# State updates of an mLSTM decoder kernel by whole units: four products of 32 rows in place of four with masked keys

## The chip, the cores and the metric

The kernel runs on one NeuronCore of a Trainium2 chip. Its time is the device time of one execution in microseconds; the median of several runs is compared. TensorE (matmuls and weight loads), VectorE, ScalarE, GpSimdE and SyncE each work through a queue of their own in order; the orders are fixed when the kernel is compiled. Results of matmuls land in PSUM, which has eight banks of 128 partitions by 512 fp32 values.

## What is computed

One inference step of a decoder with two layers, a short gated convolution and an mLSTM block, for a prompt of 512 tokens and for 8 sample sequences of 8 tokens, all in fp32. What matters here is the matrix memory of the sample sequences. Each of the 8 sequences and 4 heads has a state C of 512 x 512. In one step of 8 tokens it becomes

```python
decay = jnp.exp(g + m - m_new)
kw = kj * jnp.exp(logw - m_new[..., None])[..., None]
C_new = decay[..., None, None] * C + jnp.einsum('bhjd,bhje->bhde', kw, vj)
```

and the output of the step needs the product of the queries with the old state, `einsum('bhid,bhde->bhie', qj, C)`. That is 32 states of 1 MB to be read, used, updated and written back.

## The kernel before

**Layout.** Tokens of the samples are stacked in 32-row groups: of a head's 8 sequences, four make one half u (0 or 1), and each of the four has 32 partitions, g = 0 to 3. The 8 tokens of a sequence stand there four times, as high and low parts of key and value, so that one matmul over 32 rows gives a product of fp32 precision out of operands in a rounded fp32 format (`stack`, `value_stack`, `key_stack`). A unit (h, u, dt) is 128 of the 512 rows of C for the four sequences of a half; there are 4 x 2 x 4 = 32 units, in the order of heads 2, 0, 1, 3.

**Products.** The stationary operand has all 128 partitions, thus four sequences at once. To have one sequence alone, `key_stack` (L1166) makes four masked copies `km` of the weighted keys on ScalarE, each with one group's rows kept and the others zeroed (L1181 and L1182). `piece` (L1210) takes half a unit, two sequences: per sequence one matmul of 128 rows into a bank `r` (L1235), then one VectorE instruction that multiplies the old state by its decay and adds the bank (L1236).

**Banks.** In the last stage four PSUM banks (tag `b1`, handed out by `bank`, L133) serve these products, the query products, the decay scores (`d`), the transposes of a head's output (`ha`, `hb`) and small sums (`pn`, `qn`). Four more make the two wide accumulators of the large products.

**Queries.** `query_state` (L853) multiplies the queries with the old states: four matmuls of 32 columns each per unit (L859), which accumulate over a head's 8 units in one bank `qa`. Heads 3, 0 and 1 are done earlier in the kernel; head 2 is done in the last stage, each unit ahead of its update.

**Order.** The pieces stand in a queue, `stream`. `tick` (L195) is told of TensorE's time by the large products (0.735 us a step of eight, 0.7 in the numerators and final states) and issues a piece whenever 3.45 us have gathered. Around the pieces run the products with the gate weights `z`, the numerators, the final states of the prompt, and the output projection; their weights come by SyncE's queue, ScalarE rounds them (`wh`, L215) and VectorE computes the remainder (`wl`, L216), into four buffers each of half a chunk. A planner with a cost model fixes each engine's order from this program; instructions in a block of high priority go first when they are ready.

**Transfers.** States come in halves of 512 KB into six buffers (tag `C`). A piece issues the load of the second half after it (`load_half`, L1190; SyncE, L178) and, behind its first update, the store of the half before (`store_half`, L1200; L1205). SyncE's queue also holds the weights' loads (L221) and the other fetches (L1147).

Of the kernel before, what the change touches and what calls it, by code (L numbers as in the profile page):

```python
# [40 lines left out]
CST = {}  # L41
_n = 0
for _name, _cnt in (("ident", 128), ("ones", 128), ("causal", 128), ("smask", 256), ("sel", 64),
                    ("seln", 4), ("gmask", 4), ("k_low", 1), ("v_low", 1), ("v_one", 2)):
# [13 lines left out]
FH = 2  # L58
SECOND = tuple(range(2, 16))
FI = 1  # L60
EARLY = 3.45
NEARLY = 10
SLOTS = {}
WARM = 28
KEEP = 3
# [2 lines left out]
def trunk(tc, io):  # L68
    nc = tc.nc
    ctx = ExitStack()  # L70
    with ctx:
# [103 lines left out]
        def later_load(**kw):  # L175

            with tc.issue_after(latest[0]):
                load(**kw)  # L178
# [16 lines left out]
        def tick(us):  # L195

            if clock[1] is not None:
                clock[0] += us
                while stream and clock[0] >= clock[1]:
                    clock[0] -= clock[1]  # L200
                    stream.popleft()[1]()
                    if len(stream) == 64 - NEARLY:
                        clock[1] = PACE

        def weight_tile():
# [647 lines left out]
        def query_state(st, ct, i):  # L853

            u, dt = divmod(i, 4)
            if i == 0:
                st["q"] = bank("qa")
            for g in (2, 3, 0, 1):
                nc.tensor.matmul(st["q"][32 * g:32 * g + 32, :],  # L859
                                 st["qp"][dt // 2][:, dt % 2, 128 * u + 32 * g:128 * u + 32 * g + 32],  # L860
                                 ct[g // 2][:, g % 2, :], start=(i == 0), stop=(i == 7))
            if i == 7:
                pn = bank("qn")
                nc.tensor.matmul(pn[:, 0:1], st["qn"], c("ones", 0, 1), start=True, stop=True)
                qc = T(513, name="qc")
                nc.scalar.copy(qc[:, 0:512], st["q"])
                nc.vector.tensor_copy(qc[:, 512:513], pn[:, 0:1])
                qcs[st["h"]] = qc

        def scores(st, dt):  # L870
            if dt == 0:
# [294 lines left out]
        def key_stack(h, u):  # L1166

            st = heads[h]
            raw, = fetched.pop(("ks", h, u))
            o = R(512, "kst")  # L1170
            stack(raw, G["s"][:, 1 + u, 32 + 4 * h:33 + 4 * h], c("k_low"), o)
            pn = bank("pn")
            for dt in range(4):
                nc.tensor.matmul(pn[:, 4 * dt:4 * dt + 4], o[:, 128 * dt:128 * dt + 128], seln, start=True, stop=True)
# [3 lines left out]
            nc.vector.tensor_tensor(nst[:, h, u], pn[:, 0:16].rearrange("p (d g) -> p d g", g=4), t, ALU.add)  # L1178

            st[u] = [R(512, "km") for _ in range(4)]  # L1180
            for g, t in enumerate(st[u]):  # L1181
                nc.scalar.activation(t, o.bitcast(F32), AF.Copy, scale=c("gmask", g, g + 1))  # L1182


        ORDER = (2, 0, 1, 3)
        units = [(h, u, dt) for h in ORDER for u in range(2) for dt in range(4)]
        halves = {}
        behind = []

        def load_half(n):  # L1190

            if n < 2 * len(units):
                h, u, dt = units[n // 2]
                i = n % 2
                uid[0] += 1
                t = load_tile("c", "C")
                later_load(out=t, in_=io["cs"][(h * 2 + u) * 4 + dt][:, 2 * i:2 * i + 2])
                halves[n] = t

        def store_half(after=None):  # L1200

            while behind:
                n, t = behind.pop(0)
                h, u, dt = units[n // 2]
                ins = store(out=io["cs_out"][(h * 2 + u) * 4 + dt][:, 2 * (n % 2):2 * (n % 2) + 2], in_=t).ins  # L1205
                if after is not None:
                    tc.add_manual_dep(ins, after.name, mybir.DependencyInfo(mybir.DependencyClass.NoSync,
                                                                            mybir.DependencyReason.DATA))

        def piece(n):  # L1210

            h, u, dt = units[n // 2]
            i = n % 2
            st = heads[h]
            if i == 0:
                if "vst" not in st:
                    value_stack(h)
                if u not in st:
                    key_stack(h, u)
                m = n // 8 + 1  # L1220
                j = (ORDER[m // 2], m % 2) if m < 8 else None
                if dt == 0 and j:
                    fetch(("ks", *j), kss[j[0]][:, j[1], :])
                    if j[1] == 0 and "vst" not in heads[j[0]] and ("vs", j[0]) not in fetched:
                        fetch_stack(j[0])
                if dt == 3 and j:
                    key_stack(*j)
                if h == 2:
                    query_state(st, [halves[n], halves[n + 1]], 4 * u + dt)
            load_half(n + 2)  # L1230
            kst, vst, dec, ct = st[u], st["vst"][u], G["dec"], halves.pop(n)
            o = 8 * h + 4 * u + 2 * i
            for j in range(2):
                r = bank("r")
                nc.tensor.matmul(r, kst[2 * i + j][:, 128 * dt:128 * dt + 128], vst[:, 0:512], start=True, stop=True)  # L1235
                ins = nc.vector.scalar_tensor_tensor(ct[:, j, :], ct[:, j, :], dec[:, o + j:o + j + 1], r,  # L1236
                                                     ALU.mult, ALU.add).ins
                if j == 0:
                    store_half(ins)
            behind.append((n, ct))  # L1240
            if n == 2 * len(units) - 1:
                store_half()

        stream.extend((units[n // 2][0], lambda n=n: piece(n)) for n in range(2 * len(units)))

        def finish(h):
            while any(x[0] == h for x in stream):
# [165 lines left out]
        fetch_stack(0)  # L1413
        fetch_stack(2)
        fetch(("ks", 2, 0), kss[2][:, 0, :])
        load_half(0)
        load_half(1)
# [164 lines left out]
def _consts():  # L1582
# [23 lines left out]
    put("gmask", (g[:, None] == np.arange(4)[None, :]).astype(np.float32))  # L1606
# [112 lines left out]
```

## Time and profile before

| what | value |
|---|---|
| median of 3 runs | 1655.08 us (1655.02 to 1656.1) |
| profiled execution, first to last instruction | 1654.3 us |
| TensorE busy | 1627.4 us, 98% |
| VectorE busy | 1125.8 us, 68% |
| ScalarE busy | 806.9 us, 49% |
| bytes moved | 301.61 MB, 182 GB/s on average |
| first and last product with masked keys | 1295.7 and 1613.0 us |
| products with masked keys | 128 |
| masked copies | 32, 20.7 us of ScalarE |

The page lists a group of instructions as: line, engine, operation, output<-inputs, rows*columns of the stationary operand, shape, count | busy time, mean ns of one | idle time of the engine ahead of them and what ended it. PE is TensorE's matmuls, PEld its weight loads, DVE VectorE, ACT ScalarE, SPq SyncE's queue. The ends of matmuls are modelled and they overlap, so what one costs is read from start to start. A timeline row is: start us, length us, engine, line, operation, tiles, shape, count. An fp32 matmul stands in the records twice, one of the rounded format once.

### The profile page before, as it was taken

To read this page: it belongs to the slowest core of one execution; us is meant where nothing else is said; L and a number is where in the kernel's file an instruction comes from. 1 tells how busy PE (TensorE), PEld (TensorE's weight loads), DVE (VectorE), ACT (ScalarE), POOL (GpSimd) and SP (SyncE) were. 2 spreads that over 40 slices of the span, in tenths; PEclk is the share of its full clock that TensorE was granted. 3 is DMA by queue.
4 is the path that set the end of the run, shared out by engine and by line. 5 is a ranking of instruction groups with operands and counts; after the bars stand their busy time and mean duration, and the time that the engine had idled before them with its cause. 6 is when DMAs were issued, how large, how long until landed. Compare 5 with 4: busy or idle time off the path is not lost. (4 is left out here: it accounts for less than half of the span.)

```text
span 1654.3 us, 31177 instructions
## 1 busy us (share of the span) xinstructions
PE 1627.4 (98%) x12029; PEld 1548.7 (94%) x12029; DVE 1125.8 (68%) x2124; ACT 806.9 (49%) x1622; POOL 148.8 (9%) x295
## 2 busy tenths in 40 slices
PE   9999999999999999999999999999999998999998
PEld 9999999999999999999899989899898787989997
DVE  7988898885337976555966456446458658688775
ACT  5566666653324553434645344344345456556431
POOL 1111111110001000000111010110101000000000
PEclk9999999999999999999999999999999899999999
DMA  6476666654332434535434554454556587998992
GB/s 219 111 174 167 175 168 159 175 136 148 120 120 91 149 121 128 172 119 159 156 103 151 156 177 162 142 188 140 173 190 241 186 280 262 336 341 296 359 342 103
DMA packets 121893, 301.61 MB, mean 182 GB/s; under 512 B 12656, under 2 KB 35056, under 8 KB 121744
## 3 DMA queue, kind: packets, MB, share of 16 engines
q1 hardware_dynamic: 98320, 267.61, 48.7%
q0 software_dynamic: 8064, 14.68, 5.8%
q10 hardware_dynamic: 15360, 17.32, 3.1%
q8 instruction: 94, 1.54, 0.4%
q14 instruction: 55, 0.45, 0.1%
HBM read 235.91 MB, written 63.66 MB: 181 GB/s over the span
## 5 line engine op out<-in xcount | busy, mean ns | idle before, releaser
L345 PE MATMUL p<-hi,wh 128*128 128x288 f32 x1540 | 454.4, 297 | 3.9 <-ACT p L357 1.9
L345 PE MATMUL p<-lo,wh 128*128 128x288 f32 x1540 | 452.6, 294 | 0.0
L345 PE MATMUL p<-hi,wl 128*128 128x288 f32 x1540 | 450.7, 295 | 0.2 <-DVE wl L265 0.2
L345 PEld LDWEIGHTS p<-hi,wh 128*128 128x128 f32 x1540 | 288.5, 188 | 12.7 <-DVE ws L350 4.1
L345 PEld LDWEIGHTS p<-lo,wh 128*128 128x128 f32 x1540 | 289.0, 188 | 0.0
L345 PEld LDWEIGHTS p<-hi,wl 128*128 128x128 f32 x1540 | 287.9, 188 | 0.4 <-DVE wl L265 0.4
L264 ACT CAST wh<-wr 128x512 fp32r<-128x512 f32 (+1 forms) x298 | 171.4, 578 | 215.4 <-PE p L345 123.5
L265 DVE TENSOR_TENSOR wl<-wr,wh 128x512 fp32r<-128x512 f32 (+1 forms) x298 | 185.0, 635 | 94.9 <-ACT wh L264 92.5
L235 PE MATMUL acc<-hi,wh 128*128 128x256 f32 (+1 forms) x1072 | 233.4, 298 | 1.8 <-ACT xm L711 1.0
L235 PE MATMUL acc<-lo,wh 128*128 128x256 f32 (+1 forms) x1072 | 231.9, 297 | 0.0
L235 PE MATMUL acc<-hi,wl 128*128 128x256 f32 (+1 forms) x1072 | 231.7, 297 | 0.0
L264 ACT CAST wh<-ws 128x512 fp32r<-128x512 f32 (+1 forms) x201 | 114.8, 573 | 203.8 <-PE p L345 129.6
L215 ACT CAST wh<-wr 128x512 fp32r<-128x512 f32 x170 | 104.7, 619 | 201.2 <-PE acc L235 148.1
L235 PEld LDWEIGHTS acc<-hi,wh 128*128 128x128 f32 x1072 | 180.4, 190 | 7.4 <-issue 1.6
L216 DVE TENSOR_TENSOR wl<-wr,wh 128x512 fp32r<-128x512 f32 x170 | 116.7, 689 | 98.7 <-ACT wh L215 88.6
L235 PEld LDWEIGHTS acc<-hi,wl 128*128 128x128 f32 x1072 | 179.9, 190 | 1.6 <-issue 1.3
L235 PEld LDWEIGHTS acc<-lo,wh 128*128 128x128 f32 x1072 | 179.9, 190 | 0.6 <-issue 0.2
L265 DVE TENSOR_TENSOR wl<-ws,wh 128x512 fp32r<-128x512 f32 (+1 forms) x201 | 125.5, 630 | 68.7 <-ACT wh L264 68.0
L1236 DVE SCALAR_TENSOR_TENSOR c<-c,cols,r 128x512 f32<-128x512 f32 x128 | 91.5, 743 | 27.0 <-PE r L1235 24.9
L433 PE MATMUL p<-hi,wh 128*128 128x288 f32 x496 | 109.2, 300 | 0.0
L433 PE MATMUL p<-hi,wl 128*128 128x288 f32 x496 | 107.3, 295 | 0.0
L433 PE MATMUL p<-lo,wh 128*128 128x288 f32 x496 | 107.0, 295 | 0.0
(388 smaller groups left out, 2619.1 us busy)
## 6 DMA issues: line engine op xcount, KB each, us to landing
wr<-wts SPq DMA_DIRECT2D x222, 512.0 KB, 3.6
c<-cs SPq DMA_DIRECT2D x112, 512.0 KB, 5.8
cs_out<-c SPq DMA_DIRECT2D x64, 512.0 KB, 7.5
ws<-wts SPq DMA_DIRECT2D x28, 256.0 KB, 4.5
ws<-wts POOLq DMA_DIRECT2D x28, 256.0 KB, 4.7
wr<-wts POOLq DMA_DIRECT2D x28, 256.0 KB, 4.1
x<-xcs SPq DMA_DIRECT2D x20, 288.0 KB, 4.8
x<-xT SPq DMA_DIRECT2D x16, 288.0 KB, 4.3
```

What stands on the lines that cost most here:

```text
L215: last_act[0] = nc.scalar.copy(hi, raw[:, 4 * i:4 * i + 4, :]).ins
L216: nc.vector.tensor_tensor(lo, raw[:, 4 * i:4 * i + 4, :], hi.bitcast(F32), ALU.subtract)
L235: nc.tensor.matmul(acc[:, o:o + j - i], a[:, k % 4, :], x[:, i:j], start=(first and k == 0 and p == 0), stop=(last and k == 7 and p == 2))
L264: last_act[0] = nc.scalar.copy(hi, src).ins
L265: nc.vector.tensor_tensor(lo, src, hi.bitcast(F32), ALU.subtract)
L345: nc.tensor.matmul(bank_, a[:, j, :], x, start=(start and n + j + i == 0), stop=(n == len(groups) - 1 and j == len(g) - 1 and i == 2), ski ...
L433: nc.tensor.matmul(b, a[:, k % 4, :], x[:, t:t + HT], start=bool(start) and k == 0 and i == 0, stop=(k == n - 1 and i == 2), skip_group_ch ...
L1236: ins = nc.vector.scalar_tensor_tensor(ct[:, j, :], ct[:, j, :], dec[:, o + j:o + j + 1], r, ALU.mult, ALU.add).ins
```

## The change

- The masked copies, and the constant that made them, go. `update` replaces `piece` and does a whole unit: four matmuls, one a sequence, whose stationary and moving operands are the 32 partitions of that sequence alone, thus four different row groups of the array, into four banks.
- The four banks are claimed beforehand: VectorE clears the first column of each, in an order kept over all units; every one of the four matmuls waits for the last clear and stands in a block of high priority. Four updates on VectorE follow.
- `query_state` for head 2 no longer accumulates over 8 units in one bank: each unit has a bank of its own, which ScalarE copies for the first unit and VectorE adds for the seven others.
- Loads and stores go by units (two transfers of 512 KB each): a unit issues the load of the next one, and behind its first update the stores of the one before. The pace of the queue is 6.9 us a unit.

```diff
-PACE = 3.45
+PACE = 6.9
-EARLY = 3.45
-NEARLY = 10
+EARLY = 6.9
+NEARLY = 5
...
             u, dt = divmod(i, 4)
-            if i == 0:
+            one = st["h"] not in FAR
+            if i == 0 or one:
                 st["q"] = bank("qa")
             for g in (2, 3, 0, 1):
                 nc.tensor.matmul(st["q"][32 * g:32 * g + 32, :],
                                  st["qp"][dt // 2][:, dt % 2, 128 * u + 32 * g:128 * u + 32 * g + 32],
-                                 ct[g // 2][:, g % 2, :], start=(i == 0), stop=(i == 7))
+                                 ct[g // 2][:, g % 2, :], start=(one or i == 0), stop=(one or i == 7))
+            if i == (0 if one else 7):
+                qcs[st["h"]] = T(513, name="qc")
+                nc.scalar.copy(qcs[st["h"]][:, 0:512], st["q"])
+            elif one:
+                sums = qcs[st["h"]][:, 0:512]
+                nc.vector.tensor_tensor(sums, st["q"], sums, ALU.add)
...
-            st[u] = [R(512, "km") for _ in range(4)]
-            for g, t in enumerate(st[u]):
-                nc.scalar.activation(t, o.bitcast(F32), AF.Copy, scale=c("gmask", g, g + 1))
+            st[u] = o
...
-            load_half(n + 2)
-            kst, vst, dec, ct = st[u], st["vst"][u], G["dec"], halves.pop(n)
-            o = 8 * h + 4 * u + 2 * i
-            for j in range(2):
-                r = bank("r")
-                nc.tensor.matmul(r, kst[2 * i + j][:, 128 * dt:128 * dt + 128], vst[:, 0:512], start=True, stop=True)
-                ins = nc.vector.scalar_tensor_tensor(ct[:, j, :], ct[:, j, :], dec[:, o + j:o + j + 1], r,
-                                                     ALU.mult, ALU.add).ins
-                if j == 0:
-                    store_half(ins)
...
+            cts = held.pop(n)
+            if h == 2:
+                query_state(st, cts, 4 * u + dt)
+            load_unit(n + 1)
+            kst, vst, dec = st[u], st["vst"][u], G["dec"]
+            o = 8 * h + 4 * u
+            rs = [bank("r") for _ in range(4)]
+            for r in rs:
+                with tc.issue_after(last_bank[0]) if last_bank else nullcontext():
+                    last_bank[:] = [nc.vector.memset(r[:, 0:1], 0.0).ins]
+            with tc.high_priority():
+                for g, r in enumerate(rs):
+                    s = slice(32 * g, 32 * g + 32)
+                    mul = nc.tensor.matmul(r, kst[s, 128 * dt:128 * dt + 128], vst[s, 0:512], start=True, stop=True).ins
+                    tc.add_manual_dep(mul, last_bank[0].name, mybir.DependencyInfo(mybir.DependencyClass.Sync,
+                                                                              mybir.DependencyReason.DATA))
+            for g in range(4):
+                ct = cts[g // 2][:, g % 2, :]
+                ins = nc.vector.scalar_tensor_tensor(ct, ct, dec[:, o + g:o + g + 1], rs[g], ALU.mult, ALU.add).ins
+                if g == 0:
+                    store_unit(ins)
+            behind.append((n, cts))
```

More of the change, by code (lines that the diff above doesn't have):

```diff
@@ L864, in query_state @@
                 nc.tensor.matmul(pn[:, 0:1], st["qn"], c("ones", 0, 1), start=True, stop=True)
[L865 to L868, printed above, removed]
+                nc.vector.tensor_copy(qcs[st["h"]][:, 512:513], pn[:, 0:1])
         def scores(st, dt):
@@ L1178, in key_stack @@
             nc.vector.tensor_tensor(nst[:, h, u], pn[:, 0:16].rearrange("p (d g) -> p d g", g=4), t, ALU.add)
-            st[u] = [R(512, "km") for _ in range(4)]
-            for g, t in enumerate(st[u]):
-                nc.scalar.activation(t, o.bitcast(F32), AF.Copy, scale=c("gmask", g, g + 1))
+            st[u] = o
         ORDER = (2, 0, 1, 3)
         units = [(h, u, dt) for h in ORDER for u in range(2) for dt in range(4)]
-        halves = {}
+        held = {}
         behind = []
[L1190 to L1198, printed above, removed]
@@ L1200, in store_half @@
-        def store_half(after=None):
-            while behind:
[L1203 to L1208, printed above, removed]
@@ L1246, in finish @@
+        stream.extend((units[n][0], lambda n=n: update(n)) for n in range(len(units)))
         def finish(h):
```

64 lines of the change are left out of this document (37 added, 27 removed).

## The prediction

> **What bounds the kernel now.** I read the page first: busy shares, then the chain that ended last.
>
> ```profile
> span 1654.3 us, 31177 instructions
> PE 1627.4 (98%) x12029; PEld 1548.7 (94%) x12029; DVE 1125.8 (68%) x2124; ACT 806.9 (49%) x1622; POOL 148.8 (9%) x295
> ...
> PE 20%; DVE 2%; DMA 1%; ACT 1%; issue 0%; DVEq 0%; ACTq 0%
> ```
>
> TensorE is busy 98% of the span, and the part of the chain that could be followed is nearly all TensorE: time taken from TensorE comes off the end, unless another engine fills it again. The other one that shows is VectorE: 2% of the span, 33 us. All the changed work lies in the last stage, from about 1290 us on, so I cut that stage into stretches.
>
> ```profile
> core 0: us, PE busy (x) PEld busy (x) DVE busy (x) ACT busy (x) POOL busy (x), PEclk, DMA share, GB/s
> 1290.00:1410.00 120.00, 113.25 (x721) 92.77 (x720) 79.17 (x159) 64.53 (x142) 4.12 (x13) 0.94 0.75 259
> 1410.00:1530.00 120.00, 116.18 (x834) 110.52 (x833) 94.39 (x187) 69.43 (x145) 6.64 (x15) 0.99 0.92 321
> 1530.00:1610.00 80.00, 79.52 (x578) 76.78 (x577) 59.33 (x110) 31.29 (x60) 1.38 (x2) 1.00 0.98 359
> 1610.00:1654.00 44.00, 36.98 (x285) 35.95 (x283) 24.33 (x61) 7.87 (x18) 0.00 (x0) 0.97 0.31 104
> sum 364.00, PE 345.93 PEld 316.01 DVE 257.23 ACT 173.11 POOL 12.14; mean PE 86.48 PEld 79.00 DVE 64.31 ACT 43.28 POOL 3.04
> ```
>
> TensorE leads here too, but with less room behind it than the page suggests: VectorE is busy 79% between 1410 and 1530 us, and the DMA engines 98% between 1530 and 1610. ScalarE has room everywhere. The changed work itself, from the groups and from the line of the state product:
>
> ```profile
> L1235 PE MATMUL r<-vst,km 128*128 128x512 f32 x128 | 48.9, 436 | 2.7 <-DVE c L1236 2.3 <-ACT qc L866 0.3
> L1235 PEld LDWEIGHTS r<-vst,km 128*128 128x128 f32 x128 | 23.2, 194 | 13.2 <-DVE c L1236 4.5 <-ACT wh L215 1.7 <-issue 1.7
> L1182 ACT ACTIVATE km<-kst,cst 128x512 fp32r<-128x512 f32 x32 | 20.7, 712 | 5.4 <-DVE kst L1138 4.3 <-PE cp L1290 1.0
> L1236 DVE SCALAR_TENSOR_TENSOR c<-c,cols,r 128x512 f32<-128x512 f32 x128 | 91.5, 743 | 27.0 <-PE r L1235 24.9 <-DMA cs_out<-c 2.0
> ```
>
> There are 128 products, 32 masked keys and 128 updates; a unit of four products comes every 10 us (317 us of the stage over 32). TensorE waited for a bank of VectorE's for only 6.8 us (2.3 + 4.5), VectorE for TensorE 24.9 us.
>
> **What a product costs now.** Ends of matmuls are modelled, so I go from start to start, in TensorE's timeline.
>
> ```profile
> 1302.04 0.39 PE L1235 MATMUL r<-vst,km 128*128 128x512 f32 x1
> 1302.27 0.43 PE L235 MATMUL acc<-lo,wh 128*128 128x256 f32 x2
> 1302.54 0.43 PE L235 MATMUL acc<-hi,wl 128*128 128x256 f32 x2
> ```
>
> One product between others holds TensorE 1302.27 - 1302.04 = 0.23 us; four hold 0.92 us, and 32 units 29.4 us. The neighbours confirm the rate: 576 columns in 0.27 us, about as many per us as 512 in 0.23.
>
> **The new form: four row groups.** No instruction of the profile uses 32 rows. The nearest are the matmuls of 48 rows, for what it costs to go from all rows to a part of them and back, and the query products, four groups of 32 columns, for whether four parts work together.
>
> ```profile
> 1299.57 0.43 PE L235 MATMUL acc<-hi,wh 128*128 128x256 f32 x2
> 1299.84 0.22 PE L1113 MATMUL d<-masks 128*128 128x128 f32 x1
> 1299.99 0.32 PE L1114 MATMUL d<-Rs,pick 48*128 48x128 f32 x1
> 1300.15 0.38 PE L1116 MATMUL d<-Rs,pick 48*128 48x384 f32 x1
> 1300.46 0.53 PE L235 MATMUL acc<-lo,wh 128*128 128x256 f32 x2
> 1300.83 0.43 PE L235 MATMUL acc<-hi,wl 128*128 128x256 f32 x2
> ```
> ```profile
> 1294.15 0.53 PEld L1174 LDWEIGHTS pn<-seln,kst 128*128 128x128 f32 x4
> ...
> 1303.69 0.16 PEld L859 LDWEIGHTS qa<-c,qp 128*32 128x32 f32 x8 [0.16 <-issue]
> 1304.68 0.19 PEld L1235 LDWEIGHTS r<-vst,km 128*128 128x128 f32 x1 [0.84 <-ACT wh L215]
> ```
> ```profile
> 1294.69 1.07 PE L859 MATMUL qa<-c,qp 128*32 128x512 f32 x8
> 1295.69 0.51 PE L1235 MATMUL r<-vst,km 128*128 128x512 f32 x1
> 1296.13 1.04 PE L859 MATMUL qa<-c,qp 128*32 128x512 f32 x2
> 1297.10 0.49 PE L1235 MATMUL r<-vst,km 128*128 128x512 f32 x1
> 1297.53 1.06 PE L859 MATMUL qa<-c,qp 128*32 128x512 f32 x6
> 1298.52 0.42 PE L235 MATMUL acc<-hi,wl 128*128 128x320 f32 x1
> ```
>
> *Weights.* Four weight loads in a row take 0.53 us and one 0.19, so they follow at (0.53 - 0.19) / 3 = 0.11 us. *Switch.* From 1299.84 to 1300.83 TensorE streams 128 + 128 + 384 + 512 = 1152 columns, 0.52 us at 0.23 for 512; it took 0.99. The 0.47 us beyond that are one switch in, one out and some 0.05 for the second weight load inside. I take 0.42 us for a pair of switches: twice a pause of about 0.10 and a weight load of 0.11 that nothing covers. *Together or in turn.* Eight records of the query product (four groups, two passes) hold TensorE 1.00 us; two records hold it 0.97, six 0.99. So the four column groups run together: their eight weight loads end within 0.16 us. I take the same for row groups, 0.02 us for the later starts. A unit is then 0.42 + 0.23 + 0.02 = **0.67 us** in place of 0.92; 32 x 0.25 = **8.0 us saved**. Ends: with no switch at all 32 x (0.92 - 0.25) = 21.4 us saved; wholly in turn 0.42 + 0.92 = 1.34 a unit, 13.4 us lost. I stay near the column groups, as the closer row.
>
> [...]
>
> **Query product of head 2.** It no longer holds one bank over eight units, and state products no longer fall between its four groups. Two of its eight sets are now torn: one above (x2 and x6, 1.96 us for what a whole set does in 1.00), and one in the chain:
>
> ```profile
> 1348.82 0.97 PE qa L859 x2
> 1352.16 0.99 PE qa L859 x6
> ```
>
> Undoing both saves **2.0 us**. In return VectorE gets seven additions of 128x512.
>
> **VectorE.** Added are 128 one-column clears that claim banks, and the seven additions; I found no clear of that kind, so by the nearest rows:
>
> ```profile
> L867 DVE COPY qc<-qn 128x1 f32<-128x1 f32 x4 | 0.6, 154 | 0.0
> L1178 DVE TENSOR_TENSOR nst<-pn,ns 128x16 f32<-128x16 f32 x8 | 1.4, 172 | 5.9 <-PE pn L1174 5.9
> L1126 DVE TENSOR_TENSOR S<-S,e 128x512 f32<-128x512 f32 x3 | 2.1, 688 | 0.4 <-ACT e L1123 0.4
> ```
>
> 128 x 0.154 = 19.7 us, 7 x 0.69 = 4.8 us: 24.5 us on an engine busy 257.2 of 364. Most lies under TensorE. If all 33 us that the chain gives VectorE lie in this stage, 33 / 257 = 13% of its work sets the end: **3.1 us lost**. Ends: 0, and 24.5 if it is on the path throughout. With the clears a unit has 4 x 0.743 + 4 x 0.154 = 3.6 us of VectorE in one piece, where a half unit had 1.5; the splits of weights queue behind it, covered as long as four prepared half chunks last (24 matmuls each, 3.2 us).
>
> **At nothing:** the 20.7 us of masks leave ScalarE, which is busy 173 of 364 us. Their cover was that room, and only the first of a head's keys could have held a product up (TensorE waited 0.3 us for ScalarE's qc, none for km). The copy of qc on ScalarE only moves. The same 64 + 64 transfers of 512 KB go out, in pairs, and the 128 weight loads stay 128. The pace stays too: 6.9 us for a unit is twice 3.45 for a half.
>
> **Sum:** - 8.0 - 2.0 + 3.1 = - 6.9 us. The profiled execution spans 1654.3 us; the median of the runs is 1655.08, 0.8 us above. On the median: **1648 us**.
>
> **Rivals.**
>
> *Banks without slack (slower).* All four banks are now claimed at once and released by the last of four updates, and the products are put right behind the last clear. So any moment that VectorE runs late stops TensorE in its queue, with the weights' matmuls behind the product; and the decay scores and head transposes, which draw on the same four banks, wait out a whole unit, 3.6 us, where they found a bank after one update. Before, a product needed one bank whose update lay four products back. For it: VectorE at 79%; its waits behind ScalarE and DMA are passed on. Against: VectorE waited for TensorE more (24.9 us) than the reverse (6.8), so it is mostly early. Price: one update's 0.743 us a unit is 23.8 us, less the 6.8 waited now, 17.0; with the sum 1648.2 + 17.0 = 1665. It makes the kernel slower from (6.9 + 6.8) / 32 = 0.43 us of wait a unit.
>
> *Transfers late (slower).* Six half buffers now hold three units. A load reuses buffers whose store was issued one unit before, where it was one and a half.
>
> ```profile
> SPq L178 <- DMA cs_out<-c: 80.0, 40, 7.2
> ```
> ```profile
> cs_out<-c SPq DMA_DIRECT2D x64, 512.0 KB, 7.5
> c<-cs SPq DMA_DIRECT2D x58, 512.0 KB, 6.4
> ```
>
> SyncE already stands 80.0 us before those loads, with weights and later stores behind them. A store lands after 7.5 us and a load after 6.4: 13.9 us, against the two units (20 us) between the store's issue and the use. At 98% DMA both could grow; 1.5 us late in each of the (1613 - 1450) / 10 = 16 units after 1450 us would be 24 us on VectorE, half of it, as I judge, covered by prepared weights: 1648 + 12 = 1660.
>
> *Weight loads in turn (same).* If row groups load one after another, three more loads of 0.11 stand in a unit: 0.67 + 0.31 = 0.98, 1.9 us lost in place of 8.0 gained: 1648.2 + 9.9 = 1658; with part of the 24.9 us of VectorE's waits for TensorE gone, about 1655.
>
> *More than the sum.* The 128 products ran 0.436 us each by the group's mean, with TensorE's half clock falling on some (0.94 in the first stretch): (1 - 0.94) x 120 = 7 us are lost there. If denser units keep the clock up and concurrency is fuller, 1648 - 7 - 6 = 1635.
>
> **How the numbers follow.** Forecast 50%, its own range 1641 to 1652; more than the sum 13%; weight loads in turn 14%; banks without slack 15%; late transfers 8%. From no change a measurement tells 0.2%, 3.3 us. Faster is the forecast and the better case, less its edge: 61%. Same: the weight loads and that edge, 15%. Slower: both other rivals and a tail of the weight loads, 24%. For 8 in 10 the range reaches from the better case to the bank rival: 1635 to 1664.
>
> **What would show it.** Right: four matmuls of 32 rows start within some 0.03 us of each other, and the next matmul of 128 rows starts 0.6 to 0.7 us after the first; no km on ScalarE; 128 clears of about 0.15 us; query sets of eight records, none torn. Wrong: starts 0.1 or 0.2 us apart; more than 14 us in which TensorE waits for a clear; VectorE waiting for cs loads; a span of the half clock longer than now.

## The result: 0.83% slower, not 0.4% faster

| | before | after |
|---|---|---|
| median of the runs on one chip | 1655.59 us (1655.02 to 1657.72) | 1669.87 us (1667.77 to 1671.82) |
| profiled span | 1654.3 us | 1667.0 us |
| TensorE busy | 1627.4 us | 1625.9 us |
| TensorE idle (span less busy) | 26.9 us | 41.1 us |
| mean granted clock | 0.994 | 0.983 |

The ratio of the times is 1.0083, with a 95% interval of 1.0069 to 1.0098. The forecast was 1648 us in a range of 1635 to 1664: the time lies outside, on the other side. A table below compares the two forms of the kernel in five orders of their work. There the difference runs from -20 to +14 us, so this 14 us can't be taken as the price of the new form.

From the page of the kernel after: span, busy shares, and the chain that ended last.

```profile
span 1667.0 us, 31304 instructions
PE 1625.9 (98%) x12029; PEld 1543.0 (93%) x12029; DVE 1133.5 (68%) x2259; ACT 789.2 (47%) x1590; POOL 147.9 (9%) x295
...
PE 16%; DMA 5%; DVE 1%; ACT 1%; issue 1%; SPq 0%; DVEq 0%; ACTq 0%
```

The share of TensorE still reads 98%. Span less busy says more: the span grew by 12.7 us, busy time fell by 1.5, idle time grew by 14.2.

The last stage of the kernel after, cut where the same work begins (decay scores; head 0 and its transposes; the steady products; transposes of head 2; the rest). Columns: stretch, its length, busy time of each engine with its count, granted clock, DMA share, GB/s.

```profile
1290.00:1330.00 40.00, 36.64 (x202) 27.89 (x201) 22.58 (x50) 14.66 (x31) 0.77 (x4) 0.74 0.61 212
1330.00:1416.00 86.00, 75.87 (x495) 62.97 (x495) 57.32 (x147) 43.63 (x102) 3.82 (x9) 0.90 0.72 234
1416.00:1556.00 140.00, 131.54 (x979) 124.23 (x978) 114.11 (x289) 70.21 (x149) 7.60 (x17) 0.96 0.90 314
1556.00:1580.00 24.00, 20.20 (x151) 18.56 (x150) 10.11 (x24) 3.96 (x8) 0.00 (x0) 1.00 0.96 335
1580.00:1667.00 87.00, 79.55 (x602) 75.87 (x600) 61.97 (x145) 23.74 (x48) 0.00 (x0) 0.97 0.73 262
```

The matching stretches of the kernel before:

```profile
1290.00:1325.00 35.00, 34.54 (x185) 26.07 (x184) 19.81 (x34) 14.68 (x30) 0.93 (x4) 0.85 0.61 207
1325.00:1406.00 81.00, 75.88 (x516) 64.07 (x515) 57.44 (x121) 49.26 (x111) 3.20 (x9) 0.98 0.80 274
1406.00:1547.00 141.00, 135.52 (x971) 128.08 (x970) 110.88 (x228) 79.00 (x165) 8.02 (x17) 0.99 0.93 327
1547.00:1567.00 20.00, 20.00 (x153) 19.75 (x152) 12.48 (x20) 7.88 (x16) 0.00 (x0) 1.00 1.02 359
1567.00:1654.00 87.00, 79.98 (x593) 78.03 (x591) 56.62 (x113) 22.29 (x44) 0.00 (x0) 0.98 0.64 232
```

The steady products are 1 us shorter. The three places with other work lose 5, 5 and 4 us: the decay scores of heads 0 and 1, head 0, and the transposes of head 2. There TensorE is idle for 3.4, 10.1 and 3.8 us (length less busy), where before it was 0.5, 5.1 and 0. In the steady products it is idle for 8.5 us where it was 5.5.

**The unit itself** came out as forecast. TensorE's timeline of the kernel after, a unit with nothing late:

```profile
1572.42 0.43 PE L235 MATMUL acc<-hi,wl 128*128 128x256 f32 x2
1572.69 0.43 PE L235 MATMUL acc<-hi,wh 128*128 128x256 f32 x2
1573.04 0.50 PE L1244 MATMUL r<-vst,kst 32*128 32x512 f32 x4
1573.47 0.54 PE L235 MATMUL acc<-lo,wh 128*128 128x256 f32 x2
1573.84 0.43 PE L235 MATMUL acc<-hi,wl 128*128 128x256 f32 x2
```

From 1572.69 to 1573.84 are 1.15 us, of which two pairs of large products take 0.27 each (1572.69 - 1572.42): the unit costs 0.61 us, of which some 0.08 are the pause ahead (1573.04 against 1572.96) and 0.10 the longer step behind (0.37 against 0.27). The forecast was 0.67, in place of 0.92. The four starts lie within 0.010 us; all 32 units stand whole, and 31 of them start within 0.011 us.

The query product did not come out whole everywhere. Seven of its eight sets stand in one group of eight records; one is still torn, around a decay score, and holds TensorE 0.99 + 0.98 us for what a whole set does in 1.00:

```profile
1373.21 1.06 PE L860 MATMUL qa<-c,qp 128*32 128x512 f32 x6
...
1374.71 1.04 PE L860 MATMUL qa<-c,qp 128*32 128x512 f32 x2
```

**What TensorE waited for** in the last stage of the kernel after, by the view of waits (us in total, times, longest). The view of a single line adds the wait of a weight load to that of its matmul, which is mostly the same time twice, and so gives 7.1 us for the decay scores behind an update. This view takes the matmuls alone.

```profile
PE cp L1301 <- DVE lo L1292: 4.1, 4, 1.7
PE hb L1371 <- DVE c L1249: 3.2, 2, 2.4
PE num L1301 <- DVE ld L1416: 3.0, 1, 3.0
PE ha L1380 <- ACT y L1382: 3.0, 1, 3.0
PE d L1117 <- DVE c L1249: 2.8, 4, 0.8
PE r L1244 <- DVE r L1240: 2.6, 3, 1.2
PE cp L1301 <- ACT hi L1291: 2.4, 4, 0.7
PE num L1301 <- ACT z L994: 1.4, 1, 1.4
PE acc L235 <- ACT cp L1399: 1.4, 1, 1.4
PE cp L1301 <- DVE r L1240: 1.3, 1, 1.3
```

And of the kernel before:

```profile
PE ha L1368 <- ACT y L1370: 3.0, 2, 2.7
PE r L1235 <- DVE c L1236: 2.3, 9, 0.8
PE cp L1289 <- DVE lo L1280: 1.9, 3, 1.2
...
PE ha L1368 <- DVE c L1236: 0.8, 1, 0.8
```

All such waits of the stage come to 26.4 us after and 11.8 before; the 14.6 us between them match the added idle time. Most of them are of three kinds.

- *The four banks* (a wait for an update `c` or a clear `r` by a product or a small matmul): 3.2 + 2.8 + 2.6 = 8.6 us after and 2.3 + 0.8 = 3.1 before, 5.5 us more. In the first stretch above they are nearly all of the idle time (2.1 us for `d`, 1.2 for a clear, of 3.4).
- *The two wide accumulators*, which a large product can't take before VectorE or ScalarE has read them (`ld`, `z` and `cp` are such reads): 3.0 + 1.4 + 0.2 + 1.4 + 1.3 = 7.3 us after and 1.0 before, 6.3 us more. The last row is counted here: the view puts it to a clear, but `cp` uses none of the four banks, and VectorE's sum out of an accumulator (`ld`, L1416) ends at 1543.40 us, 0.14 us ahead of the matmul.
- *Operands* that VectorE and ScalarE make (`lo`, `hi`, `kl`): 6.7 us after and 3.1 before, 3.6 us more.

Other waits are 0.8 us shorter. That the units make the second and third kind longer is shown only in part: the two longest waits for `lo` (1.7 and 1.4 us) end right behind updates of a unit in VectorE's queue, and so does the 1.3 us, but the longest wait of all, 3.0 us for `ld` at 1525.3 us, ends behind products of a head's output and no update.

**The clock.** The half clock (0.50 from 1304.2 to 1324.6 us) holds for 47.8 us of the last stage after 1296 us in the kernel after (from 20.48 us at a stretch down to 3.41) and for 17.1 us before (10.24, 3.41 and 3.41), beside the last 5 to 7 us of either. The columns streamed in it, summed over the matmuls that start there, would take 14.4 us at the full rate after and 6.7 before; at half of it they take as long again. Three sets of query products, which are not in this sum, also start in it after, and take 1.87 us each for 1.00. That makes 10.3 us more from the clock. It is a lower estimate, since the pauses of small matmuls grow as well (0.41 us from a decay score's first matmul to its second, for 0.26). If all of TensorE's busy time in these stretches, 42.9 us after and 16.8 before, were twice what it is at the full clock, it would be 13.0 us. So the 1.5 us less of busy time are 10 to 13 us more from the clock and 12 to 15 less of work, by these estimates: the forecast had 10.0 less.

### The profile page after: what moved, and what is told of

Same layout as the page of the kernel before. It is cut to its first block, busy times and chain, and to the rows that moved or that the text cites. A ratio compares the mean times of both kernels' runs of the same rounds, so it can differ in the third digit from the quotient of the medians.

```text
span 1667.0 us, 31304 instructions
## 1 busy us (share of the span) xinstructions
PE 1625.9 (98%) x12029; PEld 1543.0 (93%) x12029; DVE 1133.5 (68%) x2259; ACT 789.2 (47%) x1590; POOL 147.9 (9%) x295
```

## The experiments

Theories by their short names: *banks* (the rival: decay scores and transposes wait out a unit), *transfers* (the rival: states late), *clock* (the half clock is what costs), *row groups* (matmuls of 32 rows bring the half clock), *order* (the planner's new order happens to be a poor one, and the form is not to blame). All ratios are to the kernel before on the same chip, with a 95% interval.

### The row groups alone, undone

Every product takes all 128 rows; clears, banks, order and pace as in the kernel after.

```diff
-                    mul = nc.tensor.matmul(r, kst[s, 128 * dt:128 * dt + 128], vst[s, 0:512], start=True, stop=True).ins
+                    mul = nc.tensor.matmul(r, kst[:, 128 * dt:128 * dt + 128], vst[:, 0:512], start=True, stop=True).ins
```

> The unit form kept whole (four banks claimed, high priority, new query form, no masks), but each of the four products takes all 128 rows: the row groups alone are undone. The state products then sum four sequences, so that part of the computation is changed. [...] Theory 'banks' (units that claim all four banks make decay scores, transposes and products wait, and the idle stretches trip the clock): half clock stays at 45 us or more and the time is 1670 + 8 = 1678 us.

1680.51 us (1676.67 to 1683.93), 1.0139 [1.0122, 1.0156]: 10.6 us more than after, and TensorE busy 1637.4 us, 11.5 more. TensorE's timeline of this run:

```profile
1445.21 0.43 PE L235 MATMUL acc<-hi,wl 128*128 128x256 f32 x2
1445.48 1.09 PE L1243 MATMUL r<-vst,kst 128*128 128x512 f32 x4
1446.40 0.43 PE L235 MATMUL acc<-hi,wh 128*128 128x256 f32 x2
```

A unit of four full products takes 1446.40 - 1445.48 = 0.92 us, and 32 x (0.92 - 0.61) = 9.9 us: the row groups save what they were to save. The half clock after 1296 us stays, 51.2 us for 47.8, so matmuls of 32 rows are not what brings it. The loss is elsewhere.

### Claims and priority

The clears, the common wait and the block of high priority go; then the priority alone.

```diff
-            for r in rs:
-                with tc.issue_after(last_bank[0]) if last_bank else nullcontext():
-                    last_bank[:] = [nc.vector.memset(r[:, 0:1], 0.0).ins]
-            with tc.high_priority():
...
-                    tc.add_manual_dep(mul, last_bank[0].name, ...)
```

> The changed kernel without the clears, without the wait for the last clear and without high priority: each product takes its bank when it comes free. Theory 'banks': with less claimed at once, TensorE's waits for VectorE's banks shrink, half clock under 30 us, time 1660 us or less, though the four products may no longer start together (then 0.4 us a unit more, up to 13 us). Theory 'row groups trip the clock': half clock stays near 48 us, time 1668 to 1675 us. Theory 'transfers' (six state buffers are three units): unchanged, 1668 to 1672 us.

```diff
-            with tc.high_priority():
+            with nullcontext():
```

> The changed kernel without the block of high priority alone; claims and the common wait stay. Theory 'banks': the order of the products hardly matters, because the banks are claimed as long, 1667 to 1673 us, half clock 40 us or more. If it is the products being put right behind the last clear that stops TensorE: 1660 us or less.

Without claims 1675.78 us (1673.79 to 1679.68), 1.0121 [1.0106, 1.0136], 5.9 us worse than after: TensorE is busy for 26.8 us more and idle for 15.9 less. The products no longer stand together: in the whole stage the 128 lie in 77 groups, in place of 32. A torn group can pay as much for the change to 32 rows and back as a whole one: the single products at 1298.52 and 1299.92 us hold TensorE 0.41 and 0.42 us up to the next matmul, a pack of four 0.43. Without the priority 1669.87 us (1667.0 to 1670.72), 1.0079 [1.0064, 1.0094], no change.

So the priority is not the cause. Of the claims the run decides less: without them the idle time is 25.2 us, below the 26.9 of the kernel before, so that all of the added idle time is gone. But a TensorE that has 26.8 us more to do also gives VectorE more time, and how much of the 15.9 us is due to that is not shown.

### The stream of units begins later

Units start behind the gate products that follow the decay scores of heads 0 and 1, so these scores meet no unit. The same edit was made in the kernel before.

```diff
         z_tile((4,))
-        clock[:] = EARLY, EARLY
...
         z_tile((0, 1, 2, 3, 4, 5, 6))
+        clock[:] = EARLY, EARLY
```

> The changed kernel, but the queue of units starts two gate products later, behind the decay scores of heads 0 and 1, so that no unit stands between them. Theory 'banks': the 20.5 us of half clock from 1304 us on go or fall to the 10 us of the kernel before, and the waits there (about 4 us) go: 1670 - 10 = 1660 us. Theory 'transfers': two units fewer at the start are two more in the crowded end, 1670 to 1678 us. Theory 'row groups trip the clock': the half clock moves with the units, 1668 to 1674 us.

> The kernel before, with its queue of half units started as late as in e5_late_stream. Theory 'banks of whole units': the decay scores of heads 0 and 1 hardly met half units (10 us of half clock), so at most that is gained: 1650 to 1657 us, and whole units by row groups are still ahead at 1648.6. Rival 'the late start alone makes the gain, and whole units cost whatever they cost before': 1640 us or less, that is as far under 1656 as e5 is under 1670.

The kernel after gains 21.3 us by it: 1648.58 us (1647.91 to 1651.17), 0.9957 [0.9942, 0.9972], **faster than the kernel before**. The kernel before loses 13 by it: 1668.63 us (1667.87 to 1669.65), 1.0075 [1.0056, 1.0093]. From the page of the late start after, whose span is 1649.4 us:

```profile
PE 1613.1 (98%) x12029; PEld 1533.4 (93%) x12029; DVE 1134.1 (69%) x2259; ACT 789.1 (48%) x1590; POOL 149.4 (9%) x295
```

The late start after has 12.8 us less of busy time than the kernel after, and 4.8 us less of idle time. Most of the 12.8 us can be the clock: TensorE is busy for 19.4 us in the half clock after 1296 us, where it was 42.9, and half of the difference is 11.8 us. The long stretch of it has not gone, though; it has moved from 1304.2 to 1361.9 us. The late start's stretch of the decay scores runs dense and at the full clock; the same stretch of the kernel after stands below it.

```profile
1300.00:1320.00 20.00, 19.10 (x142) 16.11 (x142) 14.21 (x37) 11.59 (x27) 1.20 (x6) 1.00 0.47 153
```
```profile
1300.00:1320.00 20.00, 16.64 (x63) 9.36 (x61) 13.14 (x27) 8.63 (x18) 0.00 (x0) 0.60 0.67 230
```

What that stretch looks like in the kernel after, by its timeline of all engines:

```profile
1300.43 0.50 PE L1244 MATMUL r<-vst,kst 32*128 32x512 f32 x4
1300.96 0.75 DVE L1249 SCALAR_TENSOR_TENSOR c<-c,cols,r 128x512 f32<-128x512 f32 x1 [2.80 <-PE r L1244]
...
1301.76 0.33 PE L1117 MATMUL d<-masks 128*128 128x128 f32 x1 [0.83 <-DVE c L1249]
...
1302.22 2.06 DVE L1249 SCALAR_TENSOR_TENSOR c<-c,cols,r 128x512 f32<-128x512 f32 x3
...
1303.02 0.33 PE L1117 MATMUL d<-masks 128*128 128x128 f32 x1 [0.45 <-DVE c L1249]
...
1304.40 0.47 PE L1117 MATMUL d<-masks 128*128 128x128 f32 x1
```

The unit holds all four banks; the first decay score waits 0.83 us for the first update. Behind it the scores stand one after another, small matmuls of 48 and 128 rows with no large product between them. From 1304.40 us each takes 0.47 us for 0.33: the half clock.

Such a row is not new. In the kernel before, large products stand only behind the first two groups of a score's matmuls (the first of them in the rows shown with the prediction); from 1305.03 us on the scores follow each other there too, for 4 us:

```profile
1305.03 0.22 PE L1113 MATMUL d<-masks 128*128 128x128 f32 x1
...
1308.75 0.32 PE L1122 MATMUL d<-Rp,pick 48*128 48x128 f32 x1
```

There the half clock comes at 1309.8 us and holds for 10.24 us, in the kernel after at 1304.2 us and for 20.48. What the change adds at this place are the waits in the row (0.83 and 0.45 us ahead of the half clock, where before it is one of 0.46), a row that begins with the first score, and twice the time at the half clock. That the waits and the lost cover bring the longer half clock is likely, and tested in part below; these rows alone don't show it.

The kernel before with the late start waits 8.6 us for a head's output, where it is 3.0 with the early one, and twice for a key stack, 6.7 us in all, where it has no such wait. The edit thus helps one form and harms the other, so the gain can't be put down to the unit's banks alone.

### Are the transfers late?

The second half of each unit's new state is not written back.

```diff
-                for i, t in enumerate(cts):
+                for i, t in enumerate(cts[:1]):
```

> The changed kernel, but of each unit only the first of two halves of the new state is written back (the second two sequences' states are left out): 16 MB less to move, and half the buffers come free without a store. Theory 'transfers' (loads that wait for stores make VectorE and then TensorE late): 1655 us or less. Theory 'banks': 1664 to 1671 us, with the half clock from 1304 us on unchanged.

1674.55 us (1673.59 to 1677.8), 1.0114 [1.0098, 1.013]: not faster, and slower than either theory had it. The kernel after does wait for states on VectorE, and one of these waits, 4.8 us long, is what TensorE's transposes of head 2 wait behind:

```profile
DVE c L1249 <- DMA c<-cs: 9.4, 4, 4.8
```

Without half of the stores this row is gone, but TensorE now waits 7.5 us for a key stack, which it does not in the kernel after. The late start has 7.2 us of the same row and is the fastest of all. So the transfers explain a wait of TensorE of 2.4 us at one place (of the 3.8 us idle in the stretch from 1556 us), not the 14; what they are worth in all this run can't say, with the new wait in it.

### Is it the clock?

Three more matmuls of 512 columns ahead of each decay score of heads 0 and 1, 18 in all, 3.8 us of work by their columns, whose results are overwritten.

```diff
             d, e = bank("d"), T(512, name="e")
+            if h < 2:
+                for _ in range(3):
+                    nc.tensor.matmul(d, eye, masks[:, 0:512], start=True, stop=True, skip_group_check=True)
```

> The changed kernel with three extra matmuls of 512 columns ahead of each decay score of heads 0 and 1 (18 in all, 3.8 us at full clock; the scores overwrite what they leave, the result is the same). Theory 'idle windows trip the clock': with TensorE busier in those windows, the 20.5 us of half clock from 1304 us on shrink to 10 us or less, and the time to 1664 us or less in spite of the added work. Theory 'the waits themselves are the loss, the clock only follows': 1670 + 4 = 1674 us, half clock as long.

1668.7 us (1667.18 to 1670.05), 1.0075 [1.0059, 1.0091], 1.2 us less than after with 3.8 us more to do. The same stretch as above, in this run:

```profile
1300.00:1320.00 20.00, 16.92 (x78) 9.96 (x76) 10.66 (x22) 7.06 (x14) 0.00 (x0) 0.83 0.63 226
```

The clock rises from 0.60 to 0.83 there, and from 0.983 to 0.989 in the mean: the stretch of 20.48 us from 1304.2 us shrinks to 6.83 us, and all of the half clock after 1296 us from 47.8 to 30.7. So in this run denser work goes with a higher clock, as the first theory had it; the time of 1664 us or less did not come. The gain of 1.2 us is within the scatter of the runs. If the added work is counted as 3.8 us, the clock was worth some 5 us, an estimate, since part of that work may lie in waits. Idle time stays at 41.8 us. The half clock is a part of the loss, and the waits are not its consequence.

### Other banks for the small work

Decay scores and transposes take the wide accumulators' banks, so that they never wait for an update; in the kernel after, and with the late start.

```diff
-            d, e = bank("d"), T(512, name="e")
+            d, e = mm("d")[:, 0:512], T(512, name="e")
...
-                pb = bank("hb")
+                pb = mm("hb")[:, 0:512]
...
-            pa = bank("ha")
+            pa = mm("ha")[:, 0:512]
```

> The changed kernel, but the decay scores (d) and the head transposes (hb, ha) take their PSUM space from the two wide accumulators' buffers, so that units no longer share their four banks with them. Theory 'banks' (the loss comes where decay scores and transposes stand between units and each waits for the other's banks): the losses of 1296 to 1320, 1337 to 1361 and 1380 to 1416 us go, half clock under 35 us, time 1658 us or less. Rival 'order' (the planner's new order of the rest of the work costs what it costs, banks or not): within 5 us of 1670 in either direction, with other places late. Rival 'VectorE' (four updates in one piece delay everything on VectorE): unchanged, 1668 to 1672 us.

> The same on e5_late_stream. Theory 'banks': the 20.5 us of half clock from 1362 us on (units, decay scores and head 0's transposes together) shrinks, 1640 to 1646 us. Rival 'order': 1649 plus or minus 5 us.

1679.39 us (1679.05 to 1683.49), 1.0142 [1.0118, 1.0165], and 1674.39 us (1672.56 to 1676.26), 1.0106 [1.0083, 1.0129]: worse by 9.5 and 25.8 us than the kernels that they were made from, and outside every range named ahead. Now the large products share banks with the small work. This doesn't clear the banks, since it puts another shortage in place of theirs; that the shared banks are the whole cause is not shown by it either.

### Other paces, in both forms

The pace sets how much of TensorE's time passes between units. It was moved by some 4 and 9% in the kernel after and by the same share in the kernel before.

```diff
-PACE = 6.9
+PACE = 7.2
...
-EARLY = 6.9
+EARLY = 7.2
```

> The changed kernel with the pace of units at 7.2 in place of 6.9 us (4% later each), nothing else: how much does a mere shift of the units against the rest of the work move the time? Theory 'banks': units fall elsewhere between decay scores and transposes, 1660 to 1675 us. If the time stays within 2 us of 1670, the order hardly matters and the late start of e5 won by more than a shift.

> The same for the kernel before, 3.6 in place of 3.45 us a half unit. Theory 'banks': half units leave two banks for others, the shift moves the time by less than in the changed kernel, 1652 to 1661 us. Rival 'order' (any shift moves any of these kernels by 10 us): under 1650 or over 1663 us.

> The changed kernel at a pace of 6.6 us a unit. Theory 'order' (where units fall against decay scores, transposes and head ends decides, by about 10 us either way; on the average over paces the changed kernel is ahead by what row groups save, some 8 us): anywhere from 1645 to 1672 us, and with the other paces a mean below that of the kernel before. Theory 'whole units are slower in themselves': 1665 us or more, and a mean over paces above that of the kernel before.

> The kernel before at 3.3 us a half unit, the partner of 6.6 us a unit. Theory 'order': 1650 to 1670 us, the given pace of 3.45 us being a lucky one, so slower than 1656. Theory 'whole units are slower in themselves': 1650 to 1658 us.

> The changed kernel at 7.5 us a unit: theory 'order', 1645 to 1672 us; theory 'whole units are slower in themselves', 1665 us or more; and if a slower pace alone is what helped at 7.2, under 1655 us.

> The kernel before at 3.75 us a half unit, the partner of 7.5 us: theory 'order', 1652 to 1672 us and on the mean of paces behind the changed kernel; theory 'whole units are slower in themselves', 1650 to 1658 us.

Times are medians; busy and idle are TensorE's in the profiled execution, whole units against half units.

| order (pace of units / of halves) | whole units | half units | difference | busy | idle |
|---|---|---|---|---|---|
| 6.6 / 3.3 | 1673.3 [1.0092, 1.0122] | 1678.95 [1.0118, 1.0167] | -5.7 | -10.9 | +5.6 |
| 6.9 / 3.45 (the change) | 1669.87 [1.0069, 1.0098] | 1655.59 | +14.3 | -1.5 | +14.2 |
| 7.2 / 3.6 | 1656.76 [0.9993, 1.0017] | 1664.9 [1.0033, 1.0063] | -8.1 | -12.7 | +3.5 |
| 7.5 / 3.75 | 1673.86 [1.01, 1.013] | 1671.02 [1.0087, 1.0117] | +2.8 | -11.6 | +11.0 |
| late start | 1648.58 [0.9942, 0.9972] | 1668.63 [1.0056, 1.0093] | -20.1 | -14.8 | -2.9 |

Three things follow. A shift of the pace by 4% moves either form by some 3 to 23 us, as much as the change itself. The kernel before, at 3.45, is the fastest of its five orders, with the highest mean clock of them (0.994 against 0.987 to 0.990). And the mean difference of the five pairs is -3.3 us with a standard error of 5.7: whether whole units gain or lose over orders is not resolved. What is resolved is the busy time: 10.3 us less with a standard error of 2.3. It holds the clock too, and there the whole units lose: TensorE is busy in the half clock after 1296 us for 35.7 us in the mean of their five orders and for 24.6 in those of the half units. At most half of the difference, 5.6 us, is the clock's, so that the work falls by 10 to 16 us, no less than the forecast's 10.0. The idle time grows in four of five pairs, by 6.3 us in the mean with a standard error of 3.0.

Of the expectations, 'order' is borne out by the size of the shifts, but two of its ranges were too low: the whole units at 6.6 and 7.5 took 1673.3 and 1673.86 us for at most 1672, and so lie where 'whole units are slower in themselves' had them. That theory fails on the half units, 1678.95 and 1671.02 us where it had 1650 to 1658.

One thing on the pages goes with the time in these ten kernels: the share of DMA in the chain that ended last is 1 to 2% in the three fastest and 3 to 5% in the seven others, 5% in the kernel after. Beyond the ten it does not hold (2% with all rows at 1680.51 us, none without claims at 1675.78). It is a hint that late transfers have a part in the poor orders, and no more.

The waits for the banks don't follow the time. From the view of waits of the kernel at pace 7.2:

```profile
PE d L1117 <- DVE c L1249: 2.9, 4, 0.8
```

The decay scores wait for as long as in the kernel after (2.8), in a kernel 13 us faster.

### Towards a better version

From the late start: pace 7.2; no units during the gate products that stand with the decay scores of heads 2 and 3, with pace 6.4 so that the stream ends in time; and, as a second look at the row groups, all 128 rows for every product.

```diff
-            if clock[1] is not None:
+            if clock[1] is not None and not held_back:
                 clock[0] += us
...
+                held_back.append(1)
                 z_tile((1, 3, 5))
+                held_back.clear()
```

> e5_late_stream at a pace of 7.2 us, the two changes that helped the changed kernel taken together. If pace and start act on places of their own: under 1645 us. Theory 'order' (each just deals anew): 1645 to 1672 us.

> e5_late_stream, and besides no unit is issued during the gate products that carry the decay scores of heads 2 and 3; the pace is 6.4 in place of 6.9 us to catch up. Theory 'banks': the half clock of 20.5 us from 1362 us on shrinks, 1640 to 1646 us. Theory 'transfers': units pressed closer together in the crowded part cost more than is gained, 1650 us or more.

> e5_late_stream, the fastest order so far, with the row groups alone undone: each product takes all 128 rows (the state products then sum four sequences, so that part of the computation is changed). If the 10.6 us between e1_all_rows and the changed kernel are the row groups' own saving (forecast: 8.0 us), then 1648.6 + 8 to 11 = 1657 to 1660 us here. If they were a chance of the order: anything within 10 us of 1649 on either side.

Pace 7.2: 1651.2 us (1646.21 to 1655.67), 0.9968 [0.9953, 0.9984]; the two gains don't add. Held back: 1654.07 us (1651.33 to 1655.43), 0.9984 [0.9974, 0.9994]; worse than the late start alone. All rows: 1654.96 us (1653.99 to 1656.91), 0.999 [0.9978, 1.0002], 6.4 us more than the late start with TensorE busy for 5.9 more. The late start stays the best version, 0.43% faster than the kernel before; it is also the best of more orders than the kernel before was tried in.

## Why the prediction was wrong

**What bounds the kernel: right.** TensorE sets the end. But I read its 98% as little idle time to gain, and not as a state that an edit can end: the idle time alone grew by 14.2 us, more than the span (12.7).

**The switch, together or in turn: right.** 0.61 us a unit for 0.67. (The sign named for it, 0.6 to 0.7 us from the first start to the next matmul, is 0.43: the rest of the cost lies in the pause ahead and in the step behind.) Undone alone, the row groups cost 10.6 us in one order and 6.4 in another (11.5 and 5.9 by busy time; 9 and 5.5 by the ratios to the kernel before of the same time), around the 8.0 of the sum; orders being laid out anew in these runs too, that is agreement, not a measurement to a us. The rival of weight loads in turn falls: four starts within 0.010 us. The change to 32 rows and back shows in the trace as 0.08 us ahead of a unit and 0.10 behind. For a pack that stands alone among matmuls of 128 rows the gain is 0.92 / 0.61 = 1.5 times.

**The query product: half right.** One of the two torn sets is whole now, one is still torn, so some 1.0 us of the 2.0 was saved. Together with the units the work falls by 12 to 15 us by the estimates above, against 10.0. The two were not undone apart.

**The VectorE term, + 3.1: this step failed.** The work was priced too high. The kernel after's groups:

```profile
L1240 DVE MEMSET r<- 128x1 f32 x128 | 5.2, 59 | 0.9
L868 DVE TENSOR_TENSOR qc<-qa,qc 128x512 f32<-128x512 f32 x7 | 4.8, 690 | 5.4 <-PE qa L860 5.4
```

The clears take 59 ns and 5.2 us in all, not 154 ns and 19.7 us; the additions 4.8 us as said. But its effect was priced too low, and in the wrong coin. I took a share of busy time, 13%, of the added work. What grew is the time that TensorE waits for VectorE's results. TensorE's waits that end with a VectorE result, as far as they stand in the rows above, are 4.1 + 3.2 + 3.0 + 2.8 + 2.6 + 1.3 = 17.0 us, against 2.3 + 1.9 + 0.8 = 5.0 before: 12 us where the sum had 3.1. Four updates in one piece, and four banks released one by one behind them, are the reason of some of these waits, as said above; that they are the reason of all is not shown.

**"At nothing ... the pace stays too": this failed as well.** The pace stayed in us of TensorE's time, but the planner's order did not stay with it. The half clock grew by 30.7 us, which cost 10 to 13 us by the estimates above, and for which the sum had no term. So 12 to 15 us of work are off, and 14.2 of idle time and 10 to 13 of clock on: 12.7 us, the growth of the span. The sum closes on the profile; how much a given order waits, I could not have read from the rows of before.

**Banks without slack, 1665, 15%: the nearest, and half right.** Its place is right: decay scores and transposes wait for a unit's updates. Its price was for waits of the products, 17 us over 32 units; these waited 2.6 us in all. (The 6.8 us of such waits that I read in the kernel before add the wait of the weight loads to that of their matmuls; the matmuls alone waited 2.3.) Waits for the four banks grew by 5.5 us, some two fifths of the idle time (2.4 us of them behind an update that itself waited for its state). What the rival did not have are the waits for the wide accumulators and for operands, and the clock. Nor is it a constant of the form: with the late start, the same four banks and claims give a kernel faster than the one before.

**Transfers late, 1660, 8%: present, its size not settled.** 9.4 us of VectorE's waits, 2.4 us of TensorE's that can be traced to them; 7.2 us of VectorE's in the fastest kernel too. The share of DMA in the chain grew from 1% to 5%, and no run shows what that is worth.

**More than the sum, 1635, 13%: the other way round.** Units were to keep the clock up; it fell from 0.994 to 0.983. A longer half clock had been named as a sign of being wrong, and it came. No run shows the 6 us of fuller concurrency in this price: a unit costs 0.61 us for the sum's 0.67, which is 1.9 us over 32.

**The sum's 1648 and the late start's 1648.58** agree by chance as much as by reason: the same edit takes the kernel before to 1668.63.

**Open:** which feature of an order makes its waits and its half clock (each pace has other ones), what late transfers have to do with it, what the claims are worth apart from the torn packs, and what the whole units are worth over many orders.

## What to carry to other kernels

Where a planner lays out the order anew, an edit comes with a throw of the dice of 10 us and more: price the work from TensorE's busy time, the clock from its busy time at the half clock and the order from its idle time, and compare both forms in several orders before one of them is called better. Ask of each longer block what small work has to pass it, and what large work lay between that small work before. Four 32-row products in a pack pay where they replace four masked ones (0.61 for 0.92 us), but the pack must stay whole: torn, the packs cost TensorE 26.8 us more of busy time and the kernel 5.9 us, for clears that take VectorE 5.2.

## What the runs showed of the hardware

- **A row pack among full matmuls.** Four products of 32 rows start within 0.010 us and cost 0.61 us with the change in and out. In the run without claims two single ones hold TensorE nearly as long as the pack, 0.41 and 0.42 us up to the next matmul for 0.43.
- **The half clock came without a long pause.** The longest wait of TensorE in the 19 us ahead of the 20.48 us that begin at 1304.2 us in the kernel after is the one of 0.83 us shown above; up to 1300.9 us that time is filled for the most part with large products, then with small matmuls and two waits, 1.28 us in all. The half-clock stretches of the stage last 20.48, 6.83, 6.83, 3.41, 6.83 and 3.41 us in the kernel after and 10.24, 3.41 and 3.41 in the kernel before, all multiples of 3.41 us, but for the last of either, which lasts to the end. Three more matmuls of 512 columns ahead of each score cut the half clock from 47.8 to 30.7 us, while the time moved by 1.2 us.
- **A clear of one column** in a bank takes 59 ns on VectorE, against 154 ns for a copy of one column.
